# Down projection of a two-layer decoder trunk: a different order of rounding, weight sums and squares around the fifth and fourth product

## The chip, the core and the metric

The kernel runs on one core of a Trainium2 chip. The core has five engines, each with its own queue of instructions: TensorE (PE in the profile; its weight loads are PEld), VectorE (DVE), ScalarE (ACT), GpSimd (POOL) and SyncE (SP), the last of which only issues transfers here. The metric is the device time of one execution in microseconds. A compare of two kernels takes the median of several runs.

## The reference

Two layers of a decoder trunk over 512 tokens of width 1024, in float32. Each layer is a half-step feed-forward block, a mixer (a gated linear recurrence and a sliding-window attention) and a second feed-forward block, each between two RMS norms:

```python
def swiglu(h, w_gate, w_up, w_down):
    return (jax.nn.silu(h @ w_gate) * (h @ w_up)) @ w_down

for l in range(DEPTH):                      # DEPTH = 2, D_MODEL = 1024, D_FF = 2816, SEQ = 512
    h = rms_norm(x, gn[0])
    x = x + 0.5 * rms_norm(swiglu(h, w_ffn1_gate[l], w_ffn1_up[l], w_ffn1_down[l]), gn[1])
    ...
    h = rms_norm(x, gn[4])
    x = x + 0.5 * rms_norm(swiglu(h, w_ffn2_gate[l], w_ffn2_up[l], w_ffn2_down[l]), gn[5])
```

The change touches only the last product of `swiglu`, a 512 x 2816 by 2816 x 1024 product, and the norm and residual add behind it. It is run four times: two blocks in each of two layers.

## The kernel before

**Split products.** Each operand of a float32 product is split into a high half (rounded to the faster `float32r` type) and a low half (what the rounding left). A product is three matmuls, high x high, high x low and low x high (`mm3`). ACT writes high halves (a copy that rounds), DVE the low halves (a subtraction). For weights these are the tiles `whi` (L285 or L348) and `wlo` (L296 or L355), for activations tiles named `s` (ACT L424, DVE L425, in `split`). Some low halves are made without DVE (`split_dma`): ACT writes the high half (L434) and the negated operand (L435), and POOL issues a transfer that adds the operand to it (L436).

**The down projection** (`down`, with `fast` set). Its 2816 inputs are 22 rows of 128. Rows 0 to 15 go through a scheme with seven products of quarters in place of eight (`quarters`), in the order 1, 3, 7, 2, 6, 5 and, later, 4. A product has eight steps over two token tiles, so 8 x 2 x 3 = 48 matmuls of 128x512; its weights come in four items `q` = 0 to 3 of 12 matmuls each. The weights of products 6, 5 and 4 are running sums of weight quarters, made in place on DVE (`sums`, L260): product 6 adds to `b22[q]`, which product 5 uses, and product 5 adds a raw quarter `v+q` to `b12[q]`, which product 4 uses. When that sum is made, the raw quarter's buffer is given back (`leave`) and the next load is issued (`load`); there are four such buffers (`W32`). Rows 16 to 21, the rest rows, are multiplied directly: for the first half of the 1024 output columns ahead of the seven products, and for the second half, called the tail, behind product 5, with three weight units. The splits of the rest rows' activations for the tail are made in `ready`, called from the side functions of products 6 and 5.

**Order on PE** is the program's order, written by hand: product 5, the tail for token tile 0, the tail for tile 1, product 4, the tail for tile 2, the transposes of `pre.turn(0, ...)`, the tail for tile 3. **Order on the other engines** is chosen by a scheduler, except for instructions that are wrapped in `pin`, which keep the program's order among themselves. `ws.pinned` pins the roundings of weights. `next` and `whole` split a few items ahead of their use.

**Behind the product.** For a tile `t` and a column half `h`, `half(t, h)` adds the parts (L814), squares them for the norm (ACT L623) and multiplies by the gain (L817); `post(t)` calls `half(t, 1)`, takes the root (L628, ACT L629, L630), adds to the residual `xt[t]` (L834) and stores it (SP L836); `norm(t)` squares the result and scales it (L845) for the transposes. `fetch` issues eight loads of the residual (SP L723) and one of the gain row. PE's results of products are added on DVE in `add` (L912). Loads of weights are SP L240 (pieces) and L243 (whole units, the next stage's).

Of the kernel before, what the change touches and what calls it, by code (L numbers as in the profile page):

```python
# [11 lines left out]
ALU = mybir.AluOpType  # L12
# [32 lines left out]
def trunk(ctx: ExitStack, tc: tile.TileContext, xin, wall, gains, lbT, hgain, sinks, c_dist, c_mask, c_ident, out):  # L45
# [12 lines left out]
    def nm(s):  # L58
        seq[0] += 1
        return f"{s}_{seq[0]}"  # L60

    def big(dt=F32, shape=None):
        return sb.tile(shape or [P, S], dt, tag="s", name=nm("s"), bufs=SLOTS)
# [80 lines left out]
    pin = tc.keep_in_program_order  # L144
# [10 lines left out]
    class Stream:  # L155
# [98 lines left out]
        def quarter(self, it):  # L254

            q, u, v, h = it.q, it.u, it.u + it.n, (slice(0, S), slice(S, D))

            def sums(o, x, y, op):
                for c in range(2):
                    pin(nc.vector.tensor_tensor(o[c], x[c], y[c], op=op))  # L260

            def raw(i):
                self.load(i + 1)
                return [self.raw[i][:, c] for c in h]

            def leave(i):
                self.raw.pop(i)
                self.freed += 1
                self.load(self.freed + W32)

            if it.kind in ("p1", "p2"):
                w = raw((u if it.kind == "p1" else v) + q)
            elif it.kind in ("p3", "p5"):
                w = self.b22[q]
            elif it.kind == "p7":

                w = self.b12[q]
                if q == 0:
                    sums(w, w, self.b22[q], ALU.add)
            else:  # L280
                w = self.b12[q]
            it.hi = sb.tile([P, D], F32R, tag="whi", name=nm("whi"), bufs=WS)
            it.lo = sb.tile([P, D], F32R, tag="wlo", name=nm("wlo"), bufs=WS)
            for c in range(2):
                i = nc.scalar.copy(it.hi[:, h[c]], w[c])  # L285
                if self.pinned:
                    pin(i)
            if it.kind == "p7" and q + 1 < it.n:
                sums(self.b12[q + 1], self.b12[q + 1], self.b22[q + 1], ALU.add)
            elif it.kind == "p6":  # L290
                sums(self.b22[q], self.b22[q], w, ALU.add)
            elif it.kind == "p5":
                sums(self.b12[q], raw(v + q), self.b12[q], ALU.add)
                leave(v + q)
            for c in range(2):
                pin(nc.vector.tensor_tensor(it.lo[:, h[c]], w[c], it.hi[:, h[c]].bitcast(F32), op=ALU.subtract))  # L296
            if it.kind == "p7":

                sums(w, raw(u + q), w, ALU.subtract)
                leave(u + q)  # L300
            elif it.kind == "p5":
                self.b22[q] = None
            elif it.kind == "p4":
                self.b12[q] = None
            self.done += 1
            self.flight += 1

# [94 lines left out]
    ws = Stream()  # L402
# [104 lines left out]
    class First(Quarters):  # L507
# [44 lines left out]
        def sums(self):  # L552

            k = len(self.x56)
            a = []
            for i in range(2):
                f = xs[k + 4 * i]
                nc.vector.scalar_tensor_tensor(f, f, g_sb[:, 0, 0, k + 4 * i : k + 4 * i + 1], self.rb, op0=ALU.mult, op1=ALU.mult)
                a.append([f[:, c] for c in HALF])
            self.x124.append([])  # L560
            for v in (a[0][0], a[1][0], a[1][1]):
                x = big(F32R, [P, 2, S // 2])
                split(v, to=(x[:, 0, :], x[:, 1, :]))
                self.x124[k].append(x)
            for x, v in zip((self.x56, self.x37), quarter_sums(a[0][0], a[1][0], a[0][1], a[1][1])):
                x.append(pair_split(v))

        def raw(self, half, i):
            return [[x[half + i][:, j, :] for j in range(2)] for x in self.x124]
# [114 lines left out]
    def down(src, kt, l, n, nxt, fast):  # L684
# [12 lines left out]
        def ready(n):  # L697

            for i in range(2 * js[0], min(n, kt)):
                if not isinstance(src[i], tuple):  # L700
                    src[i] = split(src[i])

        def halves(w, i):
            return w.rearrange("p (m two c) -> p m two c", two=2, c=P)[:, :, i, :]
# [11 lines left out]
        def fetch():  # L716
            g = sb.tile([P, D], F32, tag="tt", name=nm("grow"), bufs=2)
            nc.sync.dma_start(g, rows_d[(l * 6 + n) * KT : (l * 6 + n + 1) * KT, :].rearrange("k p -> (k p)").partition_broadcast(P))
            grow.append(g)
            for t in range(TT):  # L720
                for h in range(2):
                    xt[t][h] = big()
                    nc.sync.dma_start(xt[t][h], x_d[t, h])  # L723
# [9 lines left out]
        if fast:  # L733
            late = Late(src)
            b22, b12 = ws.side.pop(0)
            ws.pinned = True
            for k in range(2 * js[0] + EARLY, kt):
                part[k] = split(src[k], hold=pin)
            ws.b22, ws.b12 = [], []

            def aside(b, ps):
                b.append(ws.aside(ps.pop(0)))

            for i, j in enumerate(js):
                ws.most = (2, 3, 4)[i]
                both(j, 0)
                while len(late.s) < (3, 6, 8)[i]:
                    late.sums()
                if i:
                    aside(ws.b22, b22)  # L750
                for k in (2 * j, 2 * j + 1):
                    part.pop(k, None)
            ws.pinned = False
            ws.most = AHEAD

            def side1(q):
                if b22:
                    aside(ws.b22, b22)
                if q == 3:
                    aside(ws.b12, b12)  # L760

            def side3(q):
                if b12:
                    aside(ws.b12, b12)

            def side7(q):
                for k in (2 * q, 2 * q + 1):
                    late.second(0, k)
                    if q > 1:
                        late.more(k - 4)  # L770

            def side2(q):
                if q < 2:
                    for k in (2 * q, 2 * q + 1):
                        late.more(k + 4)

            def side6(q):
                for k in (2 * q, 2 * q + 1):
                    late.second(1, k)
                if q == 3:  # L780
                    ready(2 * js[0] + 3)

            def side5(q):
                if q == 0:
                    ready(kt)
                    fetch()

            more, product = quarters(late, y, (side1, side3, side7, side2, side6, side5))
        else:
            for j in js:  # L790
                ready(2 * j + 2 + EARLY)
                both(j, 0)
            fetch()
# [14 lines left out]
        def half(t, h):  # L808

            z = y[t][h]  # L810
            if fast:
                z = more[t][h]
                if h or t > 1:
                    nc.vector.tensor_tensor(z, y[t][h], z, op=ALU.add)  # L814
            squares(z, ss[t][:, h : h + 1])
            yg[t][h] = big()
            nc.vector.tensor_tensor(yg[t][h], z, grow[0][:, h * S : (h + 1) * S], op=ALU.mult)  # L817
# [10 lines left out]
            left[0] -= 1  # L828

        def post(t):  # L830
            half(t, 1)
            rc = root(ss[t], D)
            for h in range(2):
                nc.vector.scalar_tensor_tensor(xt[t][h], yg[t][h], rc, xt[t][h], op0=ALU.mult, op1=ALU.add)  # L834
                if pre:
                    nc.sync.dma_start(x_d[t, h], xt[t][h])  # L836
# [31 lines left out]
        for t in range(TT):  # L868
            if fast and t == 2:
                product(4, [y[t][0] for t in (2, 3)], False, side=side4)  # L870
                for t in (2, 3):
                    half(t, 0)
                t = 2
            for j, b in zip(last, bs):
                for i in range(2):
                    piece(b, t, 1, j, i)
                    order.poll()
                ws.used(b)
                if pre and (t, j) == ((2, last[-1]) if fast else (3, last[TURN])):
                    pre.turn(0, lambda kp: acc() if kp < 3 else aux())  # L880
                    if not fast:
                        norm(2)
            if not fast or t > 1:
                post(t)
                after(t)
            elif t == 0:
                post(0)
        if pre:
            order.spawn(rest())
        else:  # L890
            order.until(lambda: left[0] == 0)
# [695 lines left out]
```

## Time and profile before

| what | us |
|---|---|
| median of 3 runs (lowest, highest) | 2105.69 (2104.15, 2106.84) |
| the profiled execution, its own time | 2106.48 |
| span of the profiled execution, first to last instruction | 2104.7 |
| PE busy in the span | 2077.2 |
| DVE busy | 1646.5 |
| ACT busy | 1242.6 |

The page gives busy time by engine, the waits by engine and line, and for a stretch of time the busy time, the clock granted to PE (`PEclk`, 1.00 is the full one) and what the transfers moved. A row of the timeline is: start in us from the span's start, duration, engine, line, operation, output<-inputs, count, and in brackets the idle time before it with what ended it. Rows that follow each other without a gap are merged with a count. The records of neighbouring instructions overlap a little: two DVE operations of 128x512 that follow each other take 1.29 us together in a row, but start 0.60 us apart.

### The profile page before, as it was taken

The numbers are of one execution on the slowest core, as the hardware profiler recorded it, in microseconds if no ns is written. First come the engines' busy times: TensorE is split into PE (matmuls) and PEld (weight loads), VectorE is DVE, ScalarE is ACT, GpSimd is POOL, SyncE is SP. The second block draws the span as 40 slices with busy tenths as digits, with TensorE's granted clock in tenths as the row PEclk, the third lists the DMA queues.
The fourth block names the chain that finished last, engine by engine and source line by source line (L and its number), as shares of the span: only waits on it lengthen the run. The fifth ranks groups of instructions, "written<-read, shape, count | busy, mean of one in ns | idle before, by whom it ended". The sixth has DMA issues, their size and how long they took to land.

```text
span 2104.7 us, 36506 instructions
## 1 busy us (share of the span) xinstructions
PE 2077.2 (99%) x13561; PEld 1867.3 (89%) x13561; DVE 1646.5 (78%) x2921; ACT 1242.6 (59%) x2194; POOL 257.5 (12%) x306
## 2 busy tenths in 40 slices
PE   9999998999999999999999999999999999999998
PEld 8899987877898999998799998788778989999986
DVE  5877888766776778888988878887577758787887
ACT  6556685556354556558656566854654545665683
POOL 0011140000000011113101111300000000111140
PEclk9999999999999999999999999999999999999999
DMA  8587785321236367769637878843122562787694
GB/s 246 152 190 184 176 191 181 111 71 61 81 91 210 111 150 187 187 176 208 191 103 186 193 180 194 175 178 101 51 81 61 132 188 93 183 189 187 170 202 114
DMA packets 165074, 321.78 MB, mean 153 GB/s; under 512 B 18880, under 2 KB 84896, under 8 KB 164896
## 3 DMA queue, kind: packets, MB, share of 16 engines
q1 hardware_dynamic: 122416, 228.16, 32.6%
q0 software_dynamic: 42336, 91.24, 26.0%
q8 instruction: 106, 1.74, 0.3%
q14 instruction: 72, 0.59, 0.1%
q10 hardware_dynamic: 144, 0.05, 0.0%
HBM read 213.43 MB, written 14.73 MB: 108 GB/s over the span
## 4 chain that ended last, share of the span: by engine, by line
PE 78%; DVE 3%; ACT 3%; DMA 1%; issue 1%; SPq 0%; DVEq 0%; ACTq 0%
PE acc L114 58%; PE aux L114 18%; DMA w<-wall 1%; PE aux L124 1%; ACT whi L285 1%; PE acc L124 1%; DVE s L834 1%; DVE wlo L355 1%; DVE wlo L296 1%; ACT s L435 0%; SPq L240 0%; DVE s L260 0%; ACT s L434 0%; ACT s L623 0%; DVE s L845 0%
## 5 line engine op out<-in xcount | busy, mean ns | idle before, releaser
L114 PE MATMUL acc<-s,whi 128*128 128x256 f32 (+1 forms) x4976 | 1051.7, 309 | 0.4 <-DVE s L425 0.3
L114 PEld LDWEIGHTS acc<-s,whi 128*128 128x128 f32 x4976 | 808.9, 191 | 47.5 <-issue 3.2
L114 PE MATMUL acc<-s,wlo 128*128 128x256 f32 (+1 forms) x2488 | 764.8, 307 | 0.0
L114 PEld LDWEIGHTS acc<-s,wlo 128*128 128x128 f32 x2488 | 475.2, 191 | 23.0 <-DVE wlo L355 0.4
L114 PE MATMUL acc<-whi,s 128*128 128x512 f32 x1360 | 446.7, 397 | 0.0
L348 ACT CAST whi<-w 128x1024 fp32r<-128x1024 f32 (+1 forms) x309 | 287.0, 932 | 173.0 <-PE acc L114 94.0
L348 ACT CAST whi<-tt 128x1024 fp32r<-128x1024 f32 x160 | 167.6, 1048 | 255.8 <-DVE tt L342 192.5
L114 PEld LDWEIGHTS acc<-whi,s 128*128 128x128 f32 x1360 | 258.9, 190 | 58.7 <-ACT whi L348 1.6
L355 DVE TENSOR_TENSOR wlo<-tt,whi 128x1024 fp32r<-128x1024 f32 x160 | 196.1, 1226 | 136.8 <-ACT whi L348 133.3
L353 POOL DMA_DIRECT2D wlo<-w x166 | 143.3, 863 | 1199.9 <-DVE wlo L355 504.9
L114 PE MATMUL acc<-wlo,s 128*128 128x512 f32 x680 | 269.0, 396 | 14.3 <-DVE wlo L296 14.3
L114 PE MATMUL aux<-s,whi 128*128 128x256 f32 (+1 forms) x1296 | 239.2, 285 | 0.0
L355 DVE TENSOR_TENSOR wlo<-w,whi 128x1024 fp32r<-128x1024 f32 (+1 forms) x143 | 172.6, 1214 | 82.0 <-ACT whi L348 80.5
L114 PEld LDWEIGHTS aux<-s,whi 128*128 128x128 f32 x1296 | 202.7, 192 | 1.1 <-issue 0.5
L114 PE MATMUL aux<-s,wlo 128*128 128x256 f32 (+1 forms) x648 | 184.3, 284 | 0.0
L114 PEld LDWEIGHTS acc<-wlo,s 128*128 128x128 f32 x680 | 129.6, 191 | 41.5 <-DVE wlo L296 16.0
L114 PE MATMUL aux<-whi,s 128*128 128x512 f32 x432 | 144.0, 390 | 0.0
L352 ACT ACTIVATE wlo<-w 128x1024 fp32r<-128x1024 f32 (+1 forms) x166 | 140.7, 848 | 0.0
L436 POOL DMA_DIRECT2D s<-s x128 | 111.5, 1164 | 225.0 <-ACT s L424 98.5
L114 PEld LDWEIGHTS aux<-s,wlo 128*128 128x128 f32 x648 | 124.4, 192 | 0.3
L296 DVE TENSOR_TENSOR wlo<-s,whi 128x512 fp32r<-128x512 f32 x160 | 102.7, 685 | 9.9 <-ACT whi L285 9.9
L285 ACT CAST whi<-s 128x512 fp32r<-128x512 f32 x160 | 89.6, 617 | 33.0 <-PE aux L114 21.2
(181 smaller groups left out, 2465.8 us busy)
## 6 DMA issues: line engine op xcount, KB each, us to landing
w<-wall SPq DMA_DIRECT2D x267, 512.0 KB, 3.7
wlo<-w POOLq DMA_DIRECT2D x86, 512.0 KB, 5.3
w<-wall SPq DMA_DIRECT2D x224, 128.0 KB, 3.6
wlo<-w POOLq DMA_DIRECT2D x80, 256.0 KB, 3.4
s<-wall SPq DMA_DIRECT2D x128, 128.0 KB, 4.0
s<-s POOLq DMA_DIRECT2D x64, 256.0 KB, 4.4
x_d<-s SPq DMA_DIRECT2D x48, 256.0 KB, 2.0
s<-x_d SPq DMA_DIRECT2D x48, 256.0 KB, 5.1
```

The lines of the kernel that those rows point to most:

```text
L114: nc.tensor.matmul(o, lhsT, rhs, start=start, stop=stop)
L124: nc.tensor.transpose(o, src, ident)
L285: i = nc.scalar.copy(it.hi[:, h[c]], w[c])
L296: pin(nc.vector.tensor_tensor(it.lo[:, h[c]], w[c], it.hi[:, h[c]].bitcast(F32), op=ALU.subtract))
L348: i = nc.scalar.copy(it.hi[:, c], w[:, c])
L352: self.hold(nc.scalar.mul(it.lo[:, c], w[:, c], -1.0))
L353: nc.gpsimd.dma_start(it.lo[:, c].bitcast(F32), w[:, c], accum_op=ALU.add)
L355: self.hold(nc.vector.tensor_tensor(it.lo[:, c], w[:, c], it.hi[:, c].bitcast(F32), op=ALU.subtract))
L436: nc.gpsimd.dma_start(lo.bitcast(F32), src, accum_op=ALU.add)
L834: nc.vector.scalar_tensor_tensor(xt[t][h], yg[t][h], rc, xt[t][h], op0=ALU.mult, op1=ALU.add)
```

## The change

It adds and removes no instruction. It moves these:

- In product 5, the low halves (L296) come ahead of the sum for product 4 (L260); for `q` = 3 the sum and the return of its raw buffer move into the fourth product's first item, behind its low halves.
- The rest rows' high halves (L424, in `ready`) are pinned, and from product 6 to the end of tile 1's tail all weight roundings on ACT are pinned (`ws.pinned`).
- `fetch` moves from item 0 of product 5 to item 1.
- `half(1, 1)`, tile 1's add, square and gain, moves from inside product 4 (where `post(1)` runs) to the end of tile 1's tail.

```diff
@@ quarter
-            elif it.kind == "p5":
-                sums(self.b12[q], raw(v + q), self.b12[q], ALU.add)
-                leave(v + q)
             for c in range(2):
                 pin(nc.vector.tensor_tensor(it.lo[:, h[c]], w[c], it.hi[:, h[c]].bitcast(F32), op=ALU.subtract))
...
             elif it.kind == "p5":
                 self.b22[q] = None
+                if q + 1 < it.n:
+                    sums(self.b12[q], raw(v + q), self.b12[q], ALU.add)
+                    leave(v + q)
             elif it.kind == "p4":
                 self.b12[q] = None
+                if q == 0:
+                    i = it.n - 1
+                    sums(self.b12[i], raw(v + i), self.b12[i], ALU.add)
+                    leave(v + i)
@@ down, ready
-                    src[i] = split(src[i])
+                    src[i] = split(src[i], hold=pin if fast else None)
@@ down, side6 and side5
             def side6(q):
+                ws.pinned = True
                 for k in (2 * q, 2 * q + 1):
                     late.second(1, k)
...
             def side5(q):
                 if q == 0:
                     ready(kt)
+                elif q == 1:
                     fetch()
@@ down, post
         def post(t):
-            half(t, 1)
+            if not fast or t != 1:
+                half(t, 1)
@@ down, the loop over tiles
             elif t == 0:
                 post(0)
+            else:
+                half(1, 1)
+                ws.pinned = False
```

PE's and POOL's orders stay as they were. Three places show what the scheduler made of it, all in the first of the four down projections; the other three are alike. Lines up to 291 keep their numbers in the changed kernel, L296 becomes L293, L348 and L355 become L352 and L359, L424 and L425 become L428 and L429, L723 becomes L727 and L912 becomes L922. The numbers behind names count tiles.

ACT around the end of product 5. `s_2178` and the other sources of L424 are rest rows, `whi_3652` is product 5's item 3, `w_633`, `w_638` and `w_643` are the tail's units, `whi_3764` (3760 in the change) is product 4's item 0. Before:

```order
L424 CAST s_3637<-s_2178 128x512
L285 CAST whi_3652<-s_3096 128x512
L285 CAST whi_3652<-s_3097 128x512
L348 CAST whi_3710<-w_633_3547 128x1024
L424 CAST s_3641<-s_2305 128x512
L348 CAST whi_3728<-w_638_3580 128x1024
L424 CAST s_3645<-s_2432 128x512
L424 CAST s_3677<-s_2565 128x512
L348 CAST whi_3746<-w_643_3613 128x1024
L285 CAST whi_3764<-s_3138 128x512
```

The change:

```order
L428 CAST s_3637<-s_2178 128x512
L428 CAST s_3641<-s_2305 128x512
L428 CAST s_3645<-s_2432 128x512
L285 CAST whi_3652<-s_3096 128x512
L285 CAST whi_3652<-s_3097 128x512
L428 CAST s_3673<-s_2565 128x512
L428 CAST s_3677<-s_2702 128x512
L428 CAST s_3681<-s_2841 128x512
L352 CAST whi_3688<-w_633_3549 128x1024
L352 CAST whi_3724<-w_638_3582 128x1024
L352 CAST whi_3742<-w_643_3615 128x1024
L285 CAST whi_3760<-s_3138 128x512
```

All six rest rows now stand ahead of the three tail units. Further up in the same queue, product 5's items 0 to 2 (L285) stood together ahead of the sixteen L434 and L435 of product 4's operand; now they alternate with them, four of these ahead of each item.

DVE at the same place, with product 5's item 3 as `wlo_3653`. Before:

```order
L425 TENSOR_TENSOR s_3638<-s_2178,s_3637 128x512
L912 TENSOR_TENSOR s_3162<-acc_3528,s_3162 128x512
L425 TENSOR_TENSOR s_3642<-s_2305,s_3641 128x512
L912 TENSOR_TENSOR s_3163<-acc_3529,s_3163 128x512
L425 TENSOR_TENSOR s_3646<-s_2432,s_3645 128x512
L260 TENSOR_TENSOR s_3236<-w_580_3280,s_3236 128x512
L260 TENSOR_TENSOR s_3237<-w_580_3280,s_3237 128x512
L296 TENSOR_TENSOR wlo_3653<-s_3096,whi_3652 128x512
L296 TENSOR_TENSOR wlo_3653<-s_3097,whi_3652 128x512
L912 TENSOR_TENSOR s_3420<-acc_3528,s_3420 128x512
L912 TENSOR_TENSOR s_3421<-acc_3529,s_3421 128x512
L425 TENSOR_TENSOR s_3678<-s_2565,s_3677 128x512
```

The change:

```order
L429 TENSOR_TENSOR s_3646<-s_2432,s_3645 128x512
L293 TENSOR_TENSOR wlo_3653<-s_3096,whi_3652 128x512
L293 TENSOR_TENSOR wlo_3653<-s_3097,whi_3652 128x512
L922 TENSOR_TENSOR s_3420<-acc_3528,s_3420 128x512
L922 TENSOR_TENSOR s_3421<-acc_3529,s_3421 128x512
L429 TENSOR_TENSOR s_3674<-s_2565,s_3673 128x512
L429 TENSOR_TENSOR s_3678<-s_2702,s_3677 128x512
L429 TENSOR_TENSOR s_3682<-s_2841,s_3681 128x512
L359 TENSOR_TENSOR wlo_3689<-w_633_3549,whi_3688 128x1024
L359 TENSOR_TENSOR wlo_3725<-w_638_3582,whi_3724 128x1024
L359 TENSOR_TENSOR wlo_3743<-w_643_3615,whi_3742 128x1024
L293 TENSOR_TENSOR wlo_3761<-s_3138,whi_3760 128x512
```

Ahead of item 3's low halves still stand three rest rows and two L912 adds, but no longer the sum. Behind them all three remaining rest rows precede the first tail unit (before, one did), and the sum `s_3236`, `s_3237` has gone behind product 4's item 0. Behind that come the four adds of product 5 and the rest of tile 0's and tile 1's work, with one L817 more ahead of the first residual add than before.

SP's queue of transfers at the same place (`x_d` is the residual, `s` its tiles, `w_654` and `w_664` the next stage's first weight unit, which takes the raw buffer of item 3). Before:

```order
L240 DMA w_643_3613<-wall 128x256 x4
L243 DMA w_654_3658<-wall 128x1024
L243 DMA w_674_3714<-wall 128x1024
L723 DMA s_3691<-x_d 128x512
L723 DMA s_3693<-x_d 128x512
L723 DMA s_3695<-x_d 128x512
```

The change:

```order
L240 DMA w_643_3615<-wall 128x256 x4
L727 DMA s_3705<-x_d 128x512
L727 DMA s_3707<-x_d 128x512
L727 DMA s_3709<-x_d 128x512
L243 DMA w_664_3692<-wall 128x1024
L727 DMA s_3711<-x_d 128x512
```

Three residual loads moved ahead of the next stage's weights, right behind the tail's last unit; the other five stand behind the load that waits for item 3's raw buffer.

## The prediction, made before the changed kernel was run

> **What bounds the kernel now.** I read the page first, then PE's waits, the timeline of each wait, and windows around it.
>
> ```profile
> span 2104.7 us, 36506 instructions
> PE acc L114 <- DVE wlo L296: 14.3, 4, 5.0
> 318.94 0.39 PE L114 MATMUL acc<-wlo,s 128*128 128x512 f32 x1
> 319.62 0.39 PE L114 MATMUL acc<-wlo,s 128*128 128x512 f32 x1
> 319.85 0.61 PE L114 MATMUL acc<-whi,s 128*128 128x512 f32 x2
> 325.47 0.79 PE L114 MATMUL acc<-wlo,s 128*128 128x512 f32 x1 [5.01 <-DVE wlo L296]
> 320.08:339.02 18.94, 13.93 (x50) 0.82 0.68 234
> 1017.79:1033.23 15.44, 12.76 (x50) 0.89 0.66 224
> 1362.85:1380.66 17.81, 13.40 (x50) 0.81 0.57 206
> 2059.42:2074.37 14.95, 12.72 (x50) 0.89 0.40 126
> ```
>
> PE is busy for all but 27 us of the span, so only what PE waits for can be won without removing matmuls, and its largest waits are four, one in each down projection. Each is at the same place: the second matmul of product 5's item 3, which wants that item's low halves. Unhindered, three matmuls start 319.62 - 318.94 = 0.68 us apart, 0.227 each. The four windows run from the first matmul of item 3 (0.23 behind the start of the pair at 319.85) to the first of product 4: 12 matmuls of item 3 and 36 of the tail for tiles 0 and 1, 48 x 0.2267 = 10.88 us. They take 18.94, 15.44, 17.81 and 14.95, so the places lose 8.06, 4.56, 6.93 and 4.07: **23.6 us**, not the 14.3 of the waits.
>
> The rest is clock:
>
> ```profile
> 324.60:331.40 6.80, 5.93 (x14) 0.50 0.52 162
> 2062.00:2065.40 3.40, 3.37 (x8) 0.51 0.93 323
> 1064.86:1068.30 3.44, 3.44 (x30) 1.00 0.24 61
> 2062.03 0.79 PE L114 MATMUL acc<-wlo,s 128*128 128x512 f32 x1 [2.23 <-DVE wlo L296]
> 1064.86 0.55 PE L124 MATMUL acc<-ident,s 128*128 128x128 f32 x3 [1.34 <-DVE s L845]
> ```
>
> Behind a wait of 2.23 us PE had half its clock (0.51) for about 3.4 us, behind the 5.01 for 6.8; a wait of 1.34 elsewhere left it at 1.00. So a wait costs up to 1.7 or 3.4 us more than its length, if it is longer than something between 1.34 and 2.23. [...]
>
> Why item 3 is late, in the first of the four:
>
> ```profile
> 313.26 1.14 ACT L285 CAST whi<-s 128x512 fp32r<-128x512 f32 x2
> 316.30 1.05 ACT L348 CAST whi<-w 128x1024 fp32r<-128x1024 f32 x1 [1.90 <-DMA w<-wall]
> 317.26 0.61 ACT L424 CAST s<-s 128x512 fp32r<-128x512 f32 x1
> 320.72 1.04 ACT L348 CAST whi<-w 128x1024 fp32r<-128x1024 f32 x1 [2.85 <-DMA w<-wall]
> 321.67 1.13 ACT L424 CAST s<-s 128x512 fp32r<-128x512 f32 x2
> 323.52 1.05 ACT L348 CAST whi<-w 128x1024 fp32r<-128x1024 f32 x1 [0.72 <-DMA w<-wall]
> 309.36 1.29 DVE L260 TENSOR_TENSOR s<-w,s 128x512 f32<-128x512 f32 x2
> 310.56 1.29 DVE L296 TENSOR_TENSOR wlo<-s,whi 128x512 fp32r<-128x512 f32 x2
> 316.59 0.69 DVE L425 TENSOR_TENSOR s<-s,s 128x512 fp32r<-128x512 f32 x1
> 322.32 0.69 DVE L425 TENSOR_TENSOR s<-s,s 128x512 fp32r<-128x512 f32 x1 [3.12 <-ACT s L424]
> 322.93 1.29 DVE L260 TENSOR_TENSOR s<-w,s 128x512 f32<-128x512 f32 x2
> 324.13 1.29 DVE L296 TENSOR_TENSOR wlo<-s,whi 128x512 fp32r<-128x512 f32 x2
> 327.13 1.22 DVE L355 TENSOR_TENSOR wlo<-w,whi 128x1024 fp32r<-128x1024 f32 x1
> 328.27 0.68 DVE L425 TENSOR_TENSOR s<-s,s 128x512 fp32r<-128x512 f32 x1
> ```
>
> Item 3's high halves are ready at 314.4. Its low halves wait on DVE behind the third rest row (322.32), whose high half waits on ACT behind the second tail unit (320.72), which waits for its load. Then the sum (L260) goes first as well.
>
> **The change part by part.** Nothing is added or removed, so no busy time changes; the question is when each low half is now ready. I walk DVE's new order from 309.36, where it is busy without a gap, at 0.60 us for an operation of 128x512 (310.56 - 309.36, halved) and 1.14 for one of 128x1024 (328.27 - 327.13).
>
> *Product 5.* Low halves of item 0 end at 310.6, the sum 311.8, item 1 313.0, sum 314.2, item 2 315.4, sum 316.6; three rest rows and two L912 between them 319.6; item 3 **320.8**, with no sum ahead. ACT must be ahead of this: the first L424 stood at about 312.75 (0.51 ahead of 313.26), three of them now come before item 3's high halves, which then end at 314.4 + 2 x 0.52 = 315.4; the last three L424 end at 317. All are ahead of DVE, so the gap of 3.12 is gone. PE wants item 3's low halves at 320.08 + 0.23 = 320.3: a wait of 0.5 is left.
>
> *Tail.* Two L912 and three rest rows end at 323.8, the three L355 at 325.0, 326.1 and 327.2. PE gets to the tail at 320.08 + 12 x 0.2267 + 0.5 = 323.3 and wants the first low half at 323.5: a wait of 1.4. The next units are wanted 6 matmuls (1.36 us) apart, at 326.3 and 327.7: just in time.
>
> *Product 4.* It then starts 36 matmuls on, at 332.9. Its item 0 is ready at 328.4; then the moved sum (329.6), four L912 (332.0), two L817 and an L814 (333.8), item 1 335.0, item 2 336.2. Wanted at 332.9, 335.8 and 338.6: 0.8 us to spare for item 1.
>
> ```profile
> 341.99 1.14 ACT L285 CAST whi<-s 128x512 fp32r<-128x512 f32 x2 [5.41 <-PE aux L114]
> 344.89 1.29 DVE L296 TENSOR_TENSOR wlo<-s,whi 128x512 fp32r<-128x512 f32 x2
> ```
>
> Item 3's high halves wait for product 4's item 0 to give back its buffer, so this chain moves with PE: its low halves ended at 346.1, wanted at 339.02 + 8.16 + 0.23 = 347.4. One more L817 (0.60) now stands in it and 0.7 is left. Tile 1's squares cost nothing there; without that cover each 0.60 would be a wait.
>
> *The other three places* have DVE further ahead of PE:
>
> ```profile
> 1005.54 1.28 DVE L260 TENSOR_TENSOR s<-w,s 128x512 f32<-128x512 f32 x2
> 1350.46 1.28 DVE L260 TENSOR_TENSOR s<-w,s 128x512 f32<-128x512 f32 x2
> 2046.64 1.28 DVE L260 TENSOR_TENSOR s<-w,s 128x512 f32<-128x512 f32 x2
> ```
>
> From the start of the walk to item 3's first matmul there are 10.72 us in the first place, but 1017.79 - 1005.54 = 12.25, 12.39 and 12.78 in the others. The walk needs 11.44 for item 3 (no wait) and 15.58 for the first tail unit, which is wanted 2.72 + 0.23 behind item 3's start: at 15.20, 15.34 and 15.73. Waits of 0.4, 0.3 and 0.
>
> *Transfers.* Two things move on the queues.
>
> ```profile
> 302.10 5.82 ACT L285 CAST whi<-s 128x512 fp32r<-128x512 f32 x11
> 309.52 7.11 POOL L436 DMA_DIRECT2D s<-s  x8 [6.17 <-PE acc L114]
> s<-s POOLq DMA_DIRECT2D x8, 128.0 KB, 6.5
> 324.28 4.46 SPq L243 DMA_DIRECT2D w<-wall  x2
> s<-x_d SPq DMA_DIRECT2D x48, 256.0 KB, 5.1
> ```
>
> The eight accumulating transfers of product 4's operand (POOL) were issued together from 309.5, over the tail's loads; ACT's L434 and L435 ahead of them began when the eleven casts from 302.10 were done, at 307.8; now they begin behind five of these (product 6's), at 302.1 + 5 x 0.52 = 304.7, so they start some 3 us earlier and are spread out. The sum for item 3, and with it the return of its buffer, moves from 324.1 to 329.6, so the next stage's load (L243, 324.28) and the five residual loads behind it go out 5.3 us later: by about 332, landed by 337 (5.1). Tile 1 needs its residual only behind product 4's last items, about 343: hidden, with 6 us to spare; with none, DVE's residual add would hold the transposes for tile 1.
>
> Sum: waits of 0.5 + 1.4, 0.4, 0.3 and 0 are left, 2.7 us in all (by the bounds: none, if DVE is a little quicker; twice as much and half clock in three places, 2 x 2.7 + 3 x 1.7 = 10.5). I take 2.7 without clock, since its longest piece is near the 1.34. The gain is 23.6 - 2.7 = 20.9. From the profiled execution's 2106.48 (1.8 outside the span) that is 2085.6; the median lies 0.8 lower, so **2085**.
>
> **The rivals.** *B: the tail's loads become the wait.* The third unit's buffer was free at 315.4 and ACT could round it at 323.52, 8.1 us later. It is now free at 316.6; with 8.1 again ACT ends at 325.7, and DVE wants it at 326.1. There is 0.4 us, and three residual loads of 256 KB now follow directly: 0.79 MB at the window's 234 GB/s is 3.4 us, if they share the engines with the last unit. Against it: POOL's transfers leave earlier. [...] Price: 3.4 us, less the 0.4 on ACT and the 0.5 that the third unit has to spare on PE (327.7 - 327.2), is 2.5 in each place, with half clock in one: 10 + 1.7 on top, **2097**.
>
> *C, slower: the pinned order holds ACT.* Product 5's items 0 to 2 now stand behind L434s, whose tiles come free by earlier accumulating transfers (issued from 299 to 303).
>
> ```profile
> DMA to landing us min/median/max: 2.7/4.5/9.4
> ```
>
> If those land late, ACT stands, then DVE at product 5's low halves, then PE at items 0 to 3. The high halves are ready 2.5 us ahead of DVE. Held 7 us, of the 9.4 that the longest landing took, ACT would make PE wait 4.5 in each place and lose some 3 to the clock: 30 us on top of 2082 (the median less 23.6), **2112**. It is slower than before once each place loses 5.9, so from ACT held about 6 us. For it: this landing. Against: the median is 4.5, and at 307.8 none of the L434 waited.
>
> *D, no change:* what item 3 gains comes back in product 4's items, which DVE feeds just in time (0.7 to 0.8 us). It would need 4 us and half clock in each place, while DVE's work is the same and only its gap of 3.12 goes: **2106**.
>
> **How the numbers follow.** Forecast 0.74, B 0.14, C 0.07, D 0.05. The forecast's own range is 2082 (all 23.6) to 2093 (10.5 left); with a microsecond for the spread of the runs below and most of B above, the range is 2081 to 2096, which leaves out C, D and B's worst. What can be told from no change is 0.2%, 4.2 us. Faster: the forecast and B, 0.88; within 0.2%: D, 0.05; slower: C, 0.07.
>
> **What would show it.** Right: PE's wait for L296's successor falls from 14.3 to about 0.5, a new one for the tail's low halves (L355's) of about 2 us appears, the four windows take 46 us instead of 67, PEclk is 1.00 there, and DVE has no gap between 309 and 333. Wrong: ACT's tail roundings still wait for loads past 325 and PE with them (B); a wait of DVE for L285 in product 5 (C); waits at product 4's items (D).

## The result, and the profile after

| | before | after |
|---|---|---|
| median of six runs each (lowest, highest), us | 2106.45 (2104.15, 2109.6) | 2089.33 (2088.71, 2090.36) |
| the profiled execution, its own time | 2106.48 | 2090.36 |
| its span | 2104.7 | 2088.6 |
| the four windows of the prediction, together | 67.1 | 47.5 |

The ratio is 0.9918, with a 95% interval of 0.9906 to 0.9931: 17.1 us faster by the medians, 16.1 by the two profiled executions. The forecast was 2085, 20.9 faster. Of all executions below, one of e8 (2218.2 us, granted clock 0.864 where its others have 0.997 and more) was slow, and it is left out of medians and ranges.

The lines of the kernel have shifted: L293 makes product 5's low halves (it was L296), L352 and L359 round the weight units and make their low halves (L348, L355), L428 and L429 do it for the rest rows (L424, L425), L922 adds up products (L912), L820 and L823 add and gain in `half` (L814, L817), L841 is the residual add (L834), L852 the scaling in `norm` (L845), L612 and L618 are the casts behind the transposes of `turn`.

First PE's waits, of the changed kernel: engine, line, what it waited for, us in all, times, longest.

```profile
PE acc L124 <- DVE s L852: 5.7, 3, 1.9
PE acc L124 <- DVE s L841: 2.6, 1, 2.6
PE aux L114 <- DVE wlo L359: 2.5, 4, 1.1
```

The wait for product 5's low halves, 14.3 us before, is gone. A wait for the tail's low halves has come, 2.5 us. The second largest is the one at the end of the program, as long as before. The largest, at the transposes of the next stage, has grown: there were 5.1 us in six waits before, there are 5.7 in three now. More on it below.

The four places, from the first matmul of item 3 to the first of product 4 (start:end, length, PE busy and count, clock granted, DMA share, GB/s):

```profile
320.38:332.14 11.76, 11.18 (x49) 1.00 0.74 260
1011.32:1022.83 11.51, 11.18 (x49) 1.00 0.72 251
1354.64:1367.20 12.56, 11.44 (x49) 1.00 0.77 267
2046.37:2058.05 11.68, 11.21 (x50) 1.00 0.44 158
```

They took 18.94, 15.44, 17.81 and 14.95. The clock is full in all four. Unhindered, 48 matmuls take 10.88, so in this execution 4.0 us are left of the 23.6.

In the first place, DVE and ACT of the changed kernel:

```profile
308.37 1.28 DVE L293 TENSOR_TENSOR wlo<-s,whi 128x512 fp32r<-128x512 f32 x2
...
315.59 0.69 DVE L429 TENSOR_TENSOR s<-s,s 128x512 fp32r<-128x512 f32 x1
...
317.99 0.68 DVE L429 TENSOR_TENSOR s<-s,s 128x512 fp32r<-128x512 f32 x1
318.59 1.28 DVE L293 TENSOR_TENSOR wlo<-s,whi 128x512 fp32r<-128x512 f32 x2
319.80 1.28 DVE L922 TENSOR_TENSOR s<-acc,s 128x512 f32<-128x512 f32 x2
320.99 1.89 DVE L429 TENSOR_TENSOR s<-s,s 128x512 fp32r<-128x512 f32 x3
322.80 3.49 DVE L359 TENSOR_TENSOR wlo<-w,whi 128x1024 fp32r<-128x1024 f32 x3
```

```profile
314.35 1.66 ACT L428 CAST s<-s 128x512 fp32r<-128x512 f32 x3
317.00 1.05 ACT L352 CAST whi<-w 128x1024 fp32r<-128x1024 f32 x1 [0.99 <-DMA w<-wall]
319.00 1.05 ACT L352 CAST whi<-w 128x1024 fp32r<-128x1024 f32 x1 [0.95 <-DMA w<-wall]
321.64 1.05 ACT L352 CAST whi<-w 128x1024 fp32r<-128x1024 f32 x1 [1.60 <-DMA w<-wall]
```

And PE's waits for the tail's low halves, one in each place:

```profile
324.07 0.50 PE L114 MATMUL aux<-wlo,s 128*128 128x512 f32 x1 [0.58 <-DVE wlo L359]
...
1014.77 0.50 PE L114 MATMUL aux<-wlo,s 128*128 128x512 f32 x1 [0.34 <-DVE wlo L359]
...
1359.12 0.50 PE L114 MATMUL aux<-wlo,s 128*128 128x512 f32 x1 [1.12 <-DVE wlo L359]
...
2049.94 0.50 PE L114 MATMUL aux<-wlo,s 128*128 128x512 f32 x1 [0.47 <-DVE wlo L359]
```

No row of DVE from 308.37 to the end of the tail's units has a bracket, those that are left out here included: its gap of 3.12 is gone. ACT still waits for the tail's loads, but nothing of item 3 is queued behind it any more. DVE ends item 3 at 319.8 and the first tail unit at 322.80 + 1.14 = 323.9, with work ahead of it all the time: the wait of 0.58 that is left belongs to DVE.

**What was given back.** Both programs issue the same 13,561 matmuls in one order, so the start of each can be set against the other's. The four places win 19.6 us, 16.1 are left at the end. Of the 3.5 between, 2.8 go in the stretch where the next stage begins, within some 40 us behind three of the places (0.41, 1.95 and 0.40), 0.7 in small pieces elsewhere. In that stretch PE transposes the normalised tiles 0 and 1 first, and tiles 2 and 3 later:

```profile
364.20 0.55 PE L124 MATMUL acc<-ident,s 128*128 128x128 f32 x3 [1.90 <-DVE s L852]
...
1054.87 0.55 PE L124 MATMUL acc<-ident,s 128*128 128x128 f32 x3 [1.88 <-DVE s L852]
...
1399.25 0.55 PE L124 MATMUL acc<-ident,s 128*128 128x128 f32 x3 [1.89 <-DVE s L852]
```

The waits at the second transposes were 1.36, 1.34 and 1.37. (Those at the first, 0.34 each, are gone.) Behind the middle one the clock is halved for 3.41 us; by the comparison with the other two stages that costs 1.5 us.

### The profile page after: what moved, and what is told of

Its sections match the earlier page's. It is cut to its first block, busy times and chain, and to the rows that moved or that the text cites. A ratio compares the mean times of both kernels' runs of the same rounds, so it can differ in the third digit from the quotient of the medians.

```text
span 2088.6 us, 36534 instructions
## 1 busy us (share of the span) xinstructions
PE 2071.2 (99%) x13561; PEld 1862.1 (89%) x13561; DVE 1645.3 (79%) x2921; ACT 1242.3 (59%) x2194; POOL 257.2 (12%) x306
## 4 chain that ended last, share of the span: by engine, by line
PE 87%; ACT 4%; DVE 3%; DMA 3%; issue 2%; SPq 1%; DVEq 0%; ACTq 0%
PE acc L114 64%; PE aux L114 21%; DMA w<-wall 1%; PE aux L124 1%; DVE s L260 1%; ACT whi L285 1%; ACT s L438 1%; DMA s<-wall 1%; PE acc L124 1%; ACT s L439 1%; DVE wlo L293 1%; SPq L240 1%; DVE s L429 0%; DMA s<-xin 0%; ACT s L428 0%
## 5 line engine op out<-in xcount | busy, mean ns | idle before, releaser
L114 PE MATMUL acc<-whi,s 128*128 128x512 f32 x1360 | 441.7, 393 | 0.0
L352 ACT CAST whi<-w 128x1024 fp32r<-128x1024 f32 (+1 forms) x309 | 287.1, 933 | 168.0 <-PE acc L114 90.8
L352 ACT CAST whi<-tt 128x1024 fp32r<-128x1024 f32 x160 | 167.6, 1048 | 255.8 <-DVE tt L346 195.1
L359 DVE TENSOR_TENSOR wlo<-tt,whi 128x1024 fp32r<-128x1024 f32 x160 | 196.1, 1226 | 137.0 <-ACT whi L352 134.7
L359 DVE TENSOR_TENSOR wlo<-w,whi 128x1024 fp32r<-128x1024 f32 (+1 forms) x143 | 172.0, 1214 | 81.6 <-ACT whi L352 79.7
L293 DVE TENSOR_TENSOR wlo<-s,whi 128x512 fp32r<-128x512 f32 x160 | 102.7, 685 | 9.9 <-ACT whi L285 9.9
L428 ACT CAST s<-s 128x512 fp32r<-128x512 f32 (+1 forms) x140 | 70.7, 547 | 44.8 <-DVE s L487 41.4
```

What stands on the lines that cost most here:

```text
L114: nc.tensor.matmul(o, lhsT, rhs, start=start, stop=stop)
L352: i = nc.scalar.copy(it.hi[:, c], w[:, c])
L359: self.hold(nc.vector.tensor_tensor(it.lo[:, c], w[:, c], it.hi[:, c].bitcast(F32), op=ALU.subtract))
L428: (hold or ws.hold)(nc.scalar.copy(hi, src))
```

## The experiments

Times are medians; each ratio is to the kernel before on the same chip, with its 95% interval. The last columns list PE's waits in the profiled execution, in us: at product 5's item 3 and at the tail (four places), at the first and the second transposes (three stages). "Half clock" counts stretches at half clock, without the one at the program's end.

| kernel | us | ratio | item 3 | tail | first | second | half clock |
|---|---|---|---|---|---|---|---|
| before | 2106.45 | 1 | 5.01 2.68 4.41 2.23 | none | 0.34 each | 1.34 to 1.37 | 4 |
| change | 2089.33 | 0.9918 [0.9906, 0.9931] | none | 0.58 0.34 1.12 0.47 | none | 1.88 to 1.90 | 1 |
| e1 sums only | 2097.35 | 0.9958 [0.9945, 0.997] | 3.53 0.34 0.72 0 | 1.6 in all | 1.02 1.27 1.27 | 1.33 to 1.37 | 1 |
| e2 pins only | 2091.56 | 0.9928 [0.9916, 0.9941] | 2.78 1.64 1.26 1.30 | none | 0.31 each | 1.33 to 1.36 | 0 |
| e3 squares back | 2088.77 | 0.9914 [0.9901, 0.9928] | none | 2.0 in all | 1.07 each | 1.33 to 1.36 | 0 |
| e4 loads back | 2089.43 | 0.9919 [0.9905, 0.9932] | none | 2.3 in all | none | 1.88 to 1.89 | 1 |
| e7 tile 3 first | 2084.12 | 0.9891 [0.9877, 0.9904] | none | 2.8 in all | none | 0.44 each | 0 |
| e8 rows late | 2091.21 | 0.9923 [0.9909, 0.9937] | none | 1.3 (rest rows) | none | 1.88 to 1.90 | 0 |
| e9 e7 and e8 | 2083.03 | 0.9886 [0.9871, 0.9901] | none | 1.2 (rest rows) | none | 0.42 each | 0 |
| e10 pins later | 2085.09 | 0.989 [0.9873, 0.9908] | none | 1.7 in all | none | 1.43 to 1.47 | 0 |
| e11 as e8 | 2089.56 | 0.9911 [0.9896, 0.9926] | none | 1.9 (rest rows) | none | 1.88 each | 1 |
| e12 as the change | 2087.89 | 0.9902 [0.9887, 0.9917] | none | 1.6 in all | none | 1.88 to 1.89 | 1 |
| e13 e7 and e10 | 2080.8 | 0.9876 [0.9859, 0.9893] | 0.29 once | 2.8 in all | none | none | 0 |
| e14 as e7 | 2083.73 | 0.9892 [0.9878, 0.9907] | none | 1.7 in all | none | 0.42 each | 0 |

### e1 and e2: which part removes the wait

e1 is the kernel before with the first part alone:

```diff
-            elif it.kind == "p5":
-                sums(self.b12[q], raw(v + q), self.b12[q], ALU.add)
-                leave(v + q)
...
             elif it.kind == "p5":
                 self.b22[q] = None
+                if q + 1 < it.n:
+                    sums(self.b12[q], raw(v + q), self.b12[q], ALU.add)
+                    leave(v + q)
             elif it.kind == "p4":
                 self.b12[q] = None
+                if q == 0:
+                    ...
```

> Only the first part: the kernel before, with product 4's weight sums behind product 5's low halves; nothing is pinned, and tile 1's squares and the residual loads stand where they stood. Theory: the loss is DVE standing 3.12 us for the third rest row, because ACT rounds that row behind the second tail unit. With this part alone the scheduler already puts two rest rows ahead of the second tail unit on ACT, so the gap should go without a pin: item 3's waits 0 to 0.6 us each instead of 5.01, 2.68, 4.41 and 2.23, and a time of 2088 (2086 to 2092). Rival, the parts add up: this part takes only one sum of 1.2 us off each wait, which leaves 3.8, 1.5, 3.2 and 1.0 and half clock in two or three places: about 2098.

Measured: 2097.35, the rival's number for the time, but by another split: waits of 3.53, 0.34, 0.72 and 0. In the first place ACT and DVE show why the theory's order did not help there:

```profile
312.40 1.14 ACT L285 CAST whi<-s 128x512 fp32r<-128x512 f32 x2
319.21 1.05 ACT L352 CAST whi<-w 128x1024 fp32r<-128x1024 f32 x1 [5.67 <-DMA w<-wall]
320.17 1.12 ACT L428 CAST s<-s 128x512 fp32r<-128x512 f32 x2
```

```profile
316.33 0.68 DVE L916 TENSOR_TENSOR s<-acc,s 128x512 f32<-128x512 f32 x1
320.81 0.69 DVE L429 TENSOR_TENSOR s<-s,s 128x512 fp32r<-128x512 f32 x1 [3.81 <-ACT s L428]
...
322.62 1.28 DVE L293 TENSOR_TENSOR wlo<-s,whi 128x512 fp32r<-128x512 f32 x2
```

The rest rows stand ahead of the second tail unit, but still behind the first, and that one's load came late: ACT stood 5.67 us with the rows behind it, and DVE's gap is 3.81 in place of 3.12. So the gap comes from a rounding that waits for a load ahead of a rest row that DVE needs, whichever unit it is. The four windows fall to 54.9, a gain of 12.2, and 2.5 us come back at the first transposes.

e2 is the kernel before with the pins alone:

```diff
-                    src[i] = split(src[i])
+                    src[i] = split(src[i], hold=pin if fast else None)
...
             def side6(q):
+                ws.pinned = True
...
+            else:
+                ws.pinned = False
```

> Only the second part: the kernel before, with the rest rows and the weight roundings pinned on ACT from product 6 to the end of tile 1; the sums stay ahead of the low halves, squares and residual loads stand where they stood. Theory: the gap of 3.12 us on DVE goes here too, but DVE does one sum (1.2 us) more ahead of item 3's low halves and of the tail's, so each place loses 1.2 us more than with the whole change: item 3 waits 1.7 in the first place and 0 to 0.4 in the others, the tail's first low half 1 to 2 us, half clock in up to two places: 2095 (2092 to 2098). Rival, the pins alone bring it all and the sums' place is worth nothing: 2089 to 2090. Rival, the pins bring only what the sums do not: about 2098 or more.

Measured: 2091.56, 3.4 us under the expectation, with longer waits at item 3 than expected (in this order four adds of products stand among the rest rows ahead of its low halves where the change has two, 1.2 us more) and no half clock at all. So the pins bring most of it (15.6 us), the sums alone 9.8, the two together 17 to 19: each removes part of the same wait. Without the sums' part, item 3 waits 7.0 us in all; with it, the tail waits 2.5. Of the two pins the one on the weights decides: in the built programs, pinning the rest rows alone leaves every engine's order as it was, and pinning the weights alone gives e2's order.

### e3 and e4: the squares and the residual loads

```diff
-            if not fast or t != 1:
-                half(t, 1)
+            half(t, 1)
...
-                half(1, 1)
                 ws.pinned = False
```

> The change without its third part: tile 1's squares go back behind product 4's item 1, all else as changed. They give back the three waits of 0.34 us at the first transposes of the next stage (1.0 us) by either theory. Theory 1, the waits of 1.88 us at the second transposes come from DVE, which has the same work left behind product 5 wherever it stands: they stay at 1.9 and the time is 2090 (2089 to 2092). Theory 2, they come from the order on ACT (a weight rounding between the first two and the last six of the casts behind the first transposes): here the order is the one of before, four casts first, so the waits fall back to 1.35 and the half clock in one place goes: 2087 (2086 to 2088.5).

Measured: 2088.77. The waits at the second transposes fall to 1.33 to 1.36 and no half clock is left, as theory 2 says. But the first transposes wait 1.07 each, more than the 0.34 that either theory expected. By the starts of the matmuls, each of the three stages gives back 0.71 to 0.73 us here, and 0.67 to 0.95 in e1, which moves the sums and leaves the squares too; in e2, which leaves the sums, the waits are those of before and nothing is given back. So this loss comes with the first part. The third part takes the wait from the first transposes and adds 0.5 at the second: 0.4 is left in a stage, and 1.5 more where the clock halves. In all it is worth nothing that can be measured (2089.33 with it).

```diff
                 if q == 0:
                     ready(kt)
-                elif q == 1:
                     fetch()
```

> The change without its fourth part: the eight residual loads go out at product 5's item 0 again, all ahead of the next stage's load; ACT's and DVE's orders are those of the change. Theory: the tail's loads land 2 us and more ahead of need and the residual is wanted far later, so nothing moves: 2089 (2088 to 2090.5). Rival B of the prediction: the residual loads share the DMA engines with the tail's third unit, ACT rounds it late and PE waits some 2.5 us in each place: up to 2099, with ACT waiting for DMA at the third unit.

Measured: 2089.43, no difference. The orders of ACT and DVE are those of the change, and the residual's place on SP costs nothing either way. Rival B of the prediction falls here too: with all eight residual loads directly behind the tail's, the tail's waits are 2.3 us in all.

### e7 to e9, e11 and e12: orders that take the waits away which are left

```diff
             if not fast or t > 1:
                 post(t)
-                after(t)
+                if not fast or not pre:
+                    after(t)
+                elif t == 3:
+                    after(2)
+                    after(3)
```

> The change, with tile 3's squares and residual add put ahead of tile 2's normalisation (same instructions, another order on ACT and DVE). Theory, what the change gave back is the chain on DVE and ACT at the end of the stage: ACT stands 2.57 us there, then tile 3's squares queue behind tile 2's. In the new order DVE ends the four residual adds at 50.7 where it now ends the first two of tile 2 at 48.7 and those of tile 3 at 53.0 (times after 1000 us), tile 3's first normalised half is ready at 52.5, and PE wants it at 53.0: the three waits of 1.9 us go to 0 to 0.3, the half clock behind one of them goes too, and the time is 2082.5 (2081.5 to 2084). Rival, DVE has too much work left there whatever its order: waits of 1.3 us and more stay, 2087.5 to 2089.5.

Measured: 2084.12, 5.2 us less than the change's 2089.33, and 3.8 less than its second median, 2087.89 in e12. DVE in the stage that had the half clock, first in the change, then here:

```profile
1047.27 1.42 DVE L841 SCALAR_TENSOR_TENSOR s<-s,rt,s 128x512 f32<-128x512 f32 x2
...
1054.33 0.88 DVE L852 TENSOR_SCALAR s<-s,rt 128x512 f32<-128x512 f32 x2
```

```profile
1046.50 2.74 DVE L841 SCALAR_TENSOR_TENSOR s<-s,rt,s 128x512 f32<-128x512 f32 x4
...
1049.93 0.89 DVE L852 TENSOR_SCALAR s<-s,rt 128x512 f32<-128x512 f32 x2
...
1051.50 0.88 DVE L852 TENSOR_SCALAR s<-s,rt 128x512 f32<-128x512 f32 x2
```

The four residual adds run together, the last scaling starts 5.0 us behind the first of them (1051.50 - 1046.50) instead of 7.1, and PE waits 0.44 instead of 1.88. DVE has the same work in both, so the order on DVE and ACT alone takes most of this wait away; the rival, that the amount of work sets it, falls.

```diff
                 if q == 0:
-                    ready(kt)
+                    ready(2 * js[0] + 4)
                 elif q == 1:
                     fetch()
+                elif q == 3:
+                    ready(kt)
```

> The change, with the last two rest rows put behind the tail's roundings, on ACT and DVE. Theory, the four waits for the tail's low halves (0.58, 0.34, 1.12 and 0.47 us) are two rest rows' worth of DVE (1.2 us) ahead of them: they go, and a wait of at most 0.3 us in a place for the last rows comes in their stead, so 2087.5 (2086.5 to 2088.5). Rival, the last rows become the wait, behind DVE's adds of product 5 and ACT's wait for the third load: about 1 us in each place, 2089 or more.

Measured: 2091.21 at the median, but the executions lay between 2087.36 and 2093.98, so the same program was run again (e11) beside the change (e12):

> The same program as e8, whose runs were spread too far to tell: 2087.5 (2086.5 to 2088.5) if the tail's waits of 2.5 us are worth what they last and about half comes back as waits for the last rows; 2089 or more if not.

> [...]

Measured: 2089.56 (2089.07 to 2090.34) against the change's 2087.89 (2087.02 to 2088.2). The waits for the tail's low halves go, as the theory says, and waits for the last rest rows of 0.4 to 0.8, in three of the places, come in their stead. No gain, rather a loss of 1.7; the rival was right.

e9 has the edits of e7 and e8:

> Both of these orders together. Theory: they are in different stretches of the stage, so they add up: 2081 (2080 to 2083), no wait over 0.4 us left in the four places and at the three next stages' transposes. Rival, PE arrives earlier at a chain that was just in time, and what one wins the other loses: no better than the better of the two alone.

Measured: 2083.03, 1.1 us less than e7 beside it; the ranges (2082.01 to 2083.4, 2083.26 to 2085.19) touch, and with e11 in view this is not shown to be a gain.

### e10, e13 and e14: where the pins begin

```diff
             def side6(q):
-                ws.pinned = True
                 for k in (2 * q, 2 * q + 1):
                     late.second(1, k)
                 if q == 3:
+                    ws.pinned = True
```

> The change, with the weight roundings pinned from product 6's last item on instead of its first: on ACT product 5's roundings come before all the copies that feed POOL's accumulating transfers again, so those eight go out together (309 to 316 us in the first place) instead of from 305 on; in the four places DVE's order and the rest of ACT's are those of the change. Theory, the tail's loads land late when these transfers run beside them: the third tail rounding, at 321.6 us in the first place with the change, moves 2 to 3 us back, past DVE's want for it, and PE waits up to 1 us more in a place: 2091 (2089.5 to 2093). Rival, the loads' landing hangs on something else (their own issue): ACT's third rounding stays within 1 us and the time at 2089.

Measured: 2085.09, 2.8 us less than the change beside it (e12), which neither side expected. The third tail rounding came at 322.08, 0.4 us later than the 321.64 that the expectation starts from. Counted from item 3's first matmul it came 1.1 us later than there and than in e12, less than the theory's 2 to 3, and the tail's waits did not grow by it (1.7 us in all, 1.6 in e12). So spreading POOL's transfers brings these roundings a little sooner, and PE nothing. The gain is elsewhere. ACT behind the first transposes, first of the change, then of e10:

```profile
1039.61 0.63 ACT L627 ACTIVATE s<-s 128x512 f32<-128x512 f32 x1 [1.27 <-DVE s L820]
...
1040.24 0.82 ACT L612 ACTIVATE s<-acc,g_sb 128x256 fp32r<-128x256 f32 x2
1041.30 1.06 ACT L352 CAST whi<-w 128x1024 fp32r<-128x1024 f32 x1 [0.24 <-PE acc L114]
1042.26 1.57 ACT L612 ACTIVATE s<-acc,g_sb 128x256 fp32r<-128x256 f32 x4
```

```profile
1037.43 0.63 ACT L627 ACTIVATE s<-s 128x512 f32<-128x512 f32 x1 [1.27 <-DVE s L820]
...
1038.07 1.55 ACT L612 ACTIVATE s<-acc,g_sb 128x256 fp32r<-128x256 f32 x4
1039.49 1.06 ACT L352 CAST whi<-w 128x1024 fp32r<-128x1024 f32 x1
1040.43 0.86 ACT L612 ACTIVATE s<-acc,g_sb 128x256 fp32r<-128x256 f32 x2
```

The scheduler, which places what isn't pinned, puts a weight rounding of the next stage behind two of the eight casts in the change and behind four in e10 (as before the change, and in e2 and e3). In the change ACT stands there 0.24 for PE, and the sixth cast ends 3.6 us behind the start of the first instead of 3.2; DVE's low halves and all that follows are that much later. Matmul by matmul, e10 wins 0.4 us there and 0.4 at the second transposes in each of the three stages, and the half clock (1.6).

e13 has the edits of e7 and e10, e14 is e7's program again:

> The orders of e7 and e10 together. With e10's, ACT does four casts ahead of the weight rounding behind the first transposes and the wait at the second transposes was 1.45 us; with e7's alone it was 0.44. Theory, both shorten the same chain on DVE and ACT: the waits at the second transposes are gone (0 to 0.1), the tail's waits stay near 1.7 in all: 2082.5 (2081.5 to 2083.5), 1 to 2 us less than e7 alone. Rival, e10 won by something else than that order (in the four places themselves): then its 2.8 us come on top of e7 in full: 2081 or less.

> The same program as e7 beside it on one chip: 2084 (2083 to 2085), waits of 0.44 us at the second transposes.

Measured: 2080.8 (2079.87 to 2081.96), the fastest kernel of the study, 2.9 us less than e14's 2083.73 (2083.52 to 2084.8). Its second transposes wait for nothing. The theory forgot the 0.4 at the first casts, which adds up with e7 in full: each of the three stages wins 0.9 us over e14. So the rival had the sum right, but from the same order on ACT and not from the four places.

## Why the prediction was right, and where its size was off

**The bound, the mechanism and the direction held.** The wait for item 3 went, DVE's gap went, the clock is full in the four places, and what is left waits for DVE at the tail's low halves. e1 and e2 confirm that ACT's roundings ahead of the rest rows made the gap (e2 has none, e1 one of 3.81), and e1 adds that the first tail unit does it as well as the second.

**The walk of DVE** held almost to the last digit: from the first low halves of product 5 (308.37) item 3 took 11.43 us (forecast 11.44) and the first tail unit 15.57 (15.58). What it had wrong is where DVE stands against PE when the walk starts. It took the leads over item 3's first matmul from one execution of before, 10.72, 12.25, 12.39 and 12.78; in the change's they were 12.01, 12.26, 11.22 and 12.13. The cause lies some 30 us ahead, before anything that the change moves: a weight load that ACT, then DVE, waits for. The first and the third place, before:

```profile
290.43 0.62 ACT L285 CAST whi<-w 128x512 fp32r<-128x512 f32 x1 [3.63 <-DMA w<-wall]
...
1331.51 0.62 ACT L285 CAST whi<-w 128x512 fp32r<-128x512 f32 x1 [2.33 <-DMA w<-wall]
```

and in the change:

```profile
289.43 0.62 ACT L285 CAST whi<-w 128x512 fp32r<-128x512 f32 x1 [2.44 <-DMA w<-wall]
...
1324.49 0.62 ACT L285 CAST whi<-w 128x512 fp32r<-128x512 f32 x1 [3.41 <-DMA w<-wall]
```

Counted back from item 3's first matmul, this rounding came 1.30 us sooner in the first place and 1.19 later in the third (0.01 and 0.65 in the others); the leads moved by the same amounts, within 0.02. It moves between two executions of one program too: in the third place it came 30.15 us ahead of item 3 in the change and 31.97 in e12, and PE's wait of 1.12 in the tail there is gone in e12. So item 3's wait of 0.5 did not come, the first place's tail waited 0.58 and not 1.4, the third's 1.12 and not 0.3. That the waits came to 2.5 us in all, near the forecast's 2.1 for the tail, is luck.

**The term of 2.7 us left in the four places** (its pieces add up to 2.6) counts how late PE starts. Counted so, this execution lost 0.88, 0.63, 1.68 and 0.80, in all 4.0. In e12, the same program, the four windows take 46.2 and lose 2.7, with waits in two places only; in e4, e7 and e14, which have the same order there, they lose 3.6, 4.3 and 3.1. So the term was of the right size but at the low end of what the loads ahead make of it. The loss is more than the 2.5 us that the rows list. In e2's places, at full clock, waits of 2.78 and 1.64 lengthened the window by 14.18 - 10.88 = 3.30 and 13.04 - 10.88 = 2.16, 0.52 more each:

```profile
319.80:333.98 14.18, 11.40 (x50) 1.00 0.81 294
1012.70:1025.74 13.04, 11.40 (x49) 1.00 0.87 315
```

Part of it is the row's own reading: the matmul before counts as busy for 0.39, though the next could have started 0.227 after it.

**The step that failed** is the paragraph on product 4. It followed the moved sum and tile 1's squares ("Tile 1's squares cost nothing there") up to product 4's items, found them covered, and put the rest at nothing. No wait came in product 4. But the next stage's transposes, within some 40 us, gave 2.8 us back, in e12 as well (1.98, 0.39 and 0.41): 0.4 in each of three stages and 1.5 for half clock in one. e2, which moves neither, gives nothing back; e1 and e3, which move the sums and not the squares, give back 0.67 to 0.95 in each stage. So the loss comes with the moved sums and not with the squares. Whether it comes by the 1.2 us that DVE then does later or by the order that the scheduler chose around them is not told apart; e7 and e10 change the order alone, and each wins more in these stages than was given back. Of the 4.8 us between the forecast's 20.9 and the 16.1 of the two profiled executions, 2.8 are this step, 1.3 lie in the four places and 0.7 in small pieces elsewhere.

**The clock rule** of the prediction, a wait "longer than something between 1.34 and 2.23" halves it, is wrong as a rule on length: 2.78 in e2 did not, 1.88 did in one place of three. The cases measured are listed below.

**The rivals.** B (the tail's loads): ACT did wait for them, up to 1.60, but PE's waits in the tail were for DVE, which had work ahead all the time; e4 gave the loads more company and lost nothing (2089.43 against 2089.33). C (ACT held behind POOL's copies): no wait of DVE for product 5's high halves appeared (no bracket in DVE's rows from 308.37 on). D (product 4 too late): no wait there. "Transfers" costed at nothing held (2089.43 in e4).

## What to carry to other kernels

In e1 ACT stood 5.67 us for the load of a weight unit, with rest rows that DVE needed queued behind that rounding. So what another engine needs soon belongs ahead of any work whose data are still on the way; here that order alone brought 15.6 us (e2). When a bound engine's work is reordered, follow it on until that engine has caught up: what was put off here came due again at the next stage's first transposes, and two small changes of order there brought the time to 2080.8, 7.1 to 8.5 us under the change's two medians. A forecast that takes its starting times from one execution carries that execution's loads with it: here they moved DVE by up to 1.3 us against PE, about as much as the largest wait that was forecast (1.4). A free scheduler moves instructions far from the edit; look at its order wherever the chain is tight, not only at the edited place.

## What the runs showed of the hardware

In the profiled execution of before, half clock began at 324.53, 1020.84, 1365.59 and 2061.91 and lasted 6.83, 3.41, 6.83 and 3.41 us, each beginning within a wait, of 5.01, 2.68, 4.41 and 2.23. In the change's it began at 1056.00, behind a wait of 1.88, and lasted 3.41. (Both have another stretch at the program's end.) In the 3.41 us ahead of these five starts PE was busy for 0.00, 0.75, 1.06, 1.32 and 1.53 us. The last of before, then two places of the change and two of e11 (start:end, length, PE busy and count, clock granted, DMA share, GB/s):

```profile
2058.49:2061.90 3.41, 1.32 (x6) 1.00 0.97 277
2061.91:2065.32 3.41, 3.29 (x8) 0.50 0.93 322
```

```profile
1052.59:1056.00 3.41, 1.53 (x14) 1.00 0.41 154
1056.00:1059.41 3.41, 3.41 (x18) 0.50 0.55 167
1397.34:1400.75 3.41, 1.52 (x15) 1.00 0.44 161
1400.76:1404.17 3.41, 3.41 (x31) 1.00 0.57 173
```

```profile
1053.15:1056.56 3.41, 1.53 (x15) 1.00 0.41 154
1056.57:1059.98 3.41, 3.41 (x32) 1.00 0.65 195
1394.48:1397.89 3.41, 1.53 (x14) 1.00 0.41 156
1397.90:1401.31 3.41, 3.41 (x18) 0.50 0.52 162
```

So 1.53 us of work in such a stretch had half clock behind it in one place of e11 and full clock in the other, and the change has one of each, 1.53 and 1.52. The longest wait that cost no clock is e2's 2.78 (its place, 319.80:333.98 above, has 1.00), the shortest that did is the change's 1.88, which cost 1.5 us more in one place of three. What tells these cases apart these rows do not show.

A product of 128x512 of plain float32 (`aux<-s,ones`, before, at 37.65) left two records of 592 ns, those of the rounded halves 390 to 416 each on average.
